# Two-layer hybrid decoder with experts: in a gather, both of ScalarE's writes ahead of both of VectorE's

## The chip, the cores and the metric

The kernel runs on one core of one Trainium2 chip. The metric is the device time of one execution in microseconds (us). The engines are TensorE (PE in the profile, with its weight loads as PEld), VectorE (DVE), ScalarE (ACT), GpSimd (POOL) and SyncE (SP), which issues the transfers.

## The reference, cut to what matters

There are 256 tokens of width 1024 and two layers. Each layer has a mixer and a feed-forward part. In the second layer the feed-forward part is eight experts, of which each token uses two:

```python
logits = (t @ w_router).astype(jnp.float32)
top_v, top_i = lax.top_k(logits, TOP_K)              # 2 of 8
top_w = jax.nn.softmax(top_v, axis=-1)
...
for e in range(N_EXPERTS):
    out = out + gates[:, e:e + 1] * _swiglu(t, w_g[e], w_u[e], w_d[e])
```

`_swiglu` is `(silu(t @ w_g) * (t @ w_u)) @ w_d`, with weights of 1024 x 2816, 1024 x 2816 and 2816 x 1024 for each expert, all in float32.

## The kernel before, in words

**Precision.** A float32 number is held as two parts that TensorE can multiply fast: a high part, written by ScalarE as a copy into the type float32r, and a low part, which VectorE computes as the number minus its high part. The helper `split` (L124) issues the two: ScalarE at L125, VectorE at L127. A full product is three matmuls (`mm3`, L184 high by high, L185 high token by low weight, L186 low token by high weight).

**Weights.** They stream from HBM in chunks of 1 MB (128 x 2048). `weights` (L137) issues the load on SP into a buffer `w` or `wx` and then splits it into `wr` and `wl` (every fourth chunk into `wrx` and `wlx`): one ScalarE and one VectorE instruction for each chunk. There are 33 chunks for each expert. Chunks are asked for three ahead of TensorE (`fetch`, `AHEAD = 3`); the parts stand in three slots `wr`/`wl` and one slot `wrx`/`wlx`.

**Experts.** They are sorted by how many tokens chose them and taken in four pairs p = 0 to 3, one heavy expert (up to 128 tokens) and one light one (up to 64 tokens). The heavy one costs three matmuls (L184 to L186), the light one two (L888, L889), since the high and the low parts of its 64 tokens stand beside each other in one operand of 128 columns.

**The gather.** The tokens of a pair are brought together by `pick` (L812): matmuls of the tokens with a 0/1 matrix (L821) into a PSUM bank `gb`, two slices of 128 features in one bank, columns 0 to 127 for the heavy expert's tokens and 128 to 191 for the light one's. Then `gb` is split into the tile `xg`: `xg[:, 0]` has the heavy high parts, `xg[:, 1]` the heavy low parts, `xg[:, 2]` both parts of the light tokens. One call of `pick` handles one bank, so a pair takes four calls (here: groups 0 to 3). For pair 0 the heavy and the light part are picked by separate calls. For pairs 1, 2 and 3 one call does both, so there are 3 x 4 = 12 calls with two splits.

**Order.** The program is a list of steps: a chunk's matmuls, and between them jobs such as the gather of the pair after next (`chunk`, `collect`). It is recorded in `in_order()`, which keeps TensorE, ScalarE and VectorE each in the order in which the code is written. So an instruction that waits holds up all that stands behind it on its engine. The framework adds the semaphore waits between engines from the tiles that instructions read and write, and it also keeps two engines out of one PSUM bank.

Of the kernel before, what the change touches and what calls it, by code (L numbers as in the profile page):

```python
# [8 lines left out]
F32 = mybir.dt.float32  # L9
# [3 lines left out]
AF = mybir.ActivationFunctionType  # L13
ALU = mybir.AluOpType
# [3 lines left out]
P = 128  # L18
# [7 lines left out]
FEW = 64  # L26
# [86 lines left out]
def trunk_kernel(ctx: ExitStack, tc: tile.TileContext, x, w_in, w_out, dense_w_gate, dense_w_up, dense_w_down,  # L113
                 moe_w_gate, moe_w_up, moe_w_down, final_norm_g, consts, decay_w, out):
    nc = tc.nc
# [8 lines left out]
    def split(src, r, l, scale=1.0):  # L124
        i0 = nc.scalar.activation(r, src, AF.Copy, scale=scale)  # L125
        if isinstance(scale, float) and scale == 1.0:
            i1 = nc.vector.tensor_tensor(l, src, r.bitcast(F32), op=ALU.subtract)  # L127
        else:
            i1 = nc.vector.scalar_tensor_tensor(l, src, scale, r.bitcast(F32), op0=ALU.mult, op1=ALU.subtract)
        return i0, i1  # L130
# [66 lines left out]
    def bank(shape, name):  # L197
        return ps.tile(shape, F32, name=name, tag="ps")
# [449 lines left out]
    def moe(l, j, accs):  # L648
# [7 lines left out]
        for tt in range(TT):  # L656
            for nh in range(2):
# [4 lines left out]
                for kt in range(4 * nh, 4 * nh + 4):  # L662
# [4 lines left out]
                                   op=ALU.subtract)  # L667
# [144 lines left out]
        def pick(p, c0, c1, groups=range(KT // 2)):  # L812
            xg, oh = X[p][0:2]
            for k2 in groups:
                b = bank([P, 2, 2 * P], "gb")
                for i in range(2):
                    kt = 2 * k2 + i
                    n = 0
                    for tt in range(TT):
                        for xs in (xr, xl):  # L820
                            nc.tensor.matmul(b[:, i, c0:c1], xs[:, tt, kt * P:(kt + 1) * P],  # L821
                                             oh[:, tt].rearrange("p a b -> p (a b)")[:, c0:c1],
                                             start=(n == 0), stop=(n == 3))
                            n += 1
                ks = slice(2 * k2, 2 * k2 + 2)
                if c0 == 0:
                    split(b[:, :, 0:P], xg[:, 0, ks], xg[:, 1, ks])
                if c1 > P:
                    split(b[:, :, P:P + FEW], xg[:, 2, ks, 0:FEW], xg[:, 2, ks, FEW:P])

        def space(p):
            t = tmp([P, 4, KT, P], "xg", tag="A" if p % 2 == 0 else "E", bufs=1, dt=F32R)
# [129 lines left out]
        def scale(e, nhs=(0, 1)):  # L962
            gs = X[e // 2][2][e % 2][:, 0:1]
            if 0 in nhs:
                G[e] = tmp([P, 2, 2, 512], "yg", tag="gy", bufs=1, dt=F32R)
            for nh in nhs:
                last = split(Y[e][nh], G[e][:, 0, nh], G[e][:, 1, nh], scale=gs)
            return last
# [29 lines left out]
        def collect(p):  # L998
            jobs.extend([(space, p), (marks, p, 0), (marks, p, 1)])
            jobs.extend([(factors, p, 0), (factors, p, 1), (back, p)])  # L1000
            jobs.extend((pick, p, 0, P + FEW, (k2,)) for k2 in range(KT // 2))

        count, order, assign, where, shares, limits = places()
        jobs.extend([(count,), (order,), (assign,), (where,), (marks, 0, 1), (shares,)])
        jobs.extend((pick, 0, P, P + FEW, (k2,)) for k2 in range(KT // 2))
        jobs.extend([(factors, 0, 1), (back, 0), (limits,)])
        n_pairs = len(items[0]) + LAG
# [48 lines left out]
        space(0)  # L1056
        put = marks(0, 0)
        pick(0, 0, P)
        hold(2, (msk_set, last_x), (put,))
        with behind((put,)):  # L1060
# [11 lines left out]
        low = scale(NE - 1)  # L1072
# [142 lines left out]
```

## Time and profile before

| | us |
|---|---|
| median of 3 runs | 1178.57 |
| lowest and highest of them | 1177.09 and 1180.01 |
| the profiled execution's own time | 1178.44 |
| its span (first to last instruction) | 1176.6 |
| the experts' part in it | from about 441 on |

The span is what the trace shows; 1.84 us of the profiled execution's time lie around it. Columns of rows below that come from a timeline: start in us from the span's start, duration in us, engine, line, operation, output<-inputs, shape, count, and in brackets how long the engine stood idle ahead of the row and what ended that. Matmuls overlap, so what a matmul costs is read from one start to the next.

### The profile page before, as it was taken

How to read it: one execution, taken by the hardware profiler on the slowest of the kernel's cores; microseconds unless marked ns; L12 is line 12 of the kernel's file. 1: busy time of each engine (PE TensorE's matmuls, PEld its weight loads, DVE VectorE, ACT ScalarE, POOL GpSimd, SP SyncE). 2: the span in 40 equal slices, each digit the busy share in tenths (PEclk: the TensorE clock that was granted, in tenths of full speed). 3: DMA queues.
4: the chain of work that ended last, by engine and by line, in shares of the span. 5: the costliest groups of instructions: out<-in, count | busy, mean ns of one | idle time of the engine just before them, and what ended most of it. 6: DMA issues, size and time to landing. Idle time of an engine off the chain costs nothing.

```text
span 1176.6 us, 17161 instructions
## 1 busy us (share of the span) xinstructions
PE 1135.7 (97%) x6633; PEld 989.5 (84%) x6633; DVE 991.0 (84%) x1065; ACT 788.6 (67%) x801; POOL 28.1 (2%) x36
## 2 busy tenths in 40 slices
PE   6999999999899999999989999999999999999995
PEld 6998999999799978888868888878888878888883
DVE  4998655555679876899889999979999979999996
ACT  5754544334455466688678887778887778887873
POOL 2001000000000120000000000000000000000000
PEclk9999999999999998999999999999999999999998
DMA  9333455455433455998989999989999989999991
GB/s 377 129 139 149 184 190 198 180 179 179 163 133 137 180 215 204 369 383 322 368 323 414 391 424 389 417 319 410 392 424 389 408 322 409 393 424 389 425 386 38
DMA packets 48934, 348.97 MB, mean 297 GB/s; under 512 B 5447, under 2 KB 5447, under 8 KB 7120
## 3 DMA queue, kind: packets, MB, share of 16 engines
q1 hardware_dynamic: 48384, 345.50, 74.5%
q0 software_dynamic: 464, 2.33, 0.5%
q8 instruction: 54, 0.88, 0.3%
q14 instruction: 32, 0.26, 0.1%
HBM read 346.76 MB, written 1.05 MB: 296 GB/s over the span
## 4 chain that ended last, share of the span: by engine, by line
PE 88%; DVE 5%; ACT 3%; issue 2%; DMA 1%; POOL 0%; SPq 0%; POOLq 0%; ACTq 0%; DVEq 0%
PE gu L186 10%; PE gu L184 10%; PE gu L185 10%; PE acc_y L184 6%; PE acc_y L186 6%; PE acc_y L185 6%; PE gu L888 6%; PE gu L889 6%; DVE wl L127 3%; PE acc_y L957 3%; PE fb L930 3%; PE acc_y L958 3%; PE sbk L445 1%; ACT wr L125 1%; PE a_ps L191 1%
## 5 line engine op out<-in xcount | busy, mean ns | idle before, releaser
L127 DVE TENSOR_TENSOR wl<-w,wr 128x2048 fp32r<-128x2048 f32 (+2 forms) x267 | 464.5, 1762 | 68.0 <-ACT wr L125 67.6
L125 ACT ACTIVATE wr<-w 128x2048 fp32r<-128x2048 f32 (+2 forms) x267 | 391.7, 1490 | 186.8 <-issue 108.9
L127 DVE TENSOR_TENSOR wl<-wx,wr 128x2048 fp32r<-128x2048 f32 x54 | 123.0, 2287 | 9.6 <-ACT wr L125 9.5
L186 PE MATMUL gu<-wr,xg 128*128 128x512 f32 (+1 forms) x296 | 112.5, 380 | 2.0 <-DVE xg L127 2.0
L185 PE MATMUL gu<-wl,xg 128*128 128x512 f32 (+1 forms) x296 | 112.3, 379 | 1.9 <-DVE wl L127 1.8
L184 PE MATMUL gu<-wr,xg 128*128 128x512 f32 (+1 forms) x296 | 113.9, 385 | 0.0
L125 ACT ACTIVATE wr<-wx 128x2048 fp32r<-128x2048 f32 x54 | 102.5, 1910 | 7.5 <-PE gu L186 3.4
L127 DVE TENSOR_TENSOR wlx<-w,wrx 128x2048 fp32r<-128x2048 f32 x45 | 102.8, 2286 | 5.1 <-ACT wrx L125 5.0
L888 PE MATMUL gu<-wr,xg 128*128 128x512 f32 (+1 forms) x288 | 106.4, 377 | 0.0
L889 PE MATMUL gu<-wl,xg 128*128 128x512 f32 (+1 forms) x288 | 104.5, 370 | 0.0
L184 PE MATMUL gu<-f,wr 128*128 128x256 f32 x336 | 95.1, 283 | 0.0
L185 PE MATMUL gu<-f,wr 128*128 128x256 f32 x336 | 95.0, 283 | 0.0
L186 PE MATMUL gu<-f,wl 128*128 128x256 f32 x336 | 95.0, 283 | 0.0
L185 PE MATMUL acc_y<-wl,hr 128*128 128x512 f32 x228 | 90.0, 395 | 0.6 <-DVE wl L127 0.6
L184 PE MATMUL acc_y<-wr,hr 128*128 128x512 f32 x228 | 90.3, 396 | 0.0
L186 PE MATMUL acc_y<-wr,hl 128*128 128x512 f32 x228 | 89.9, 394 | 0.0
L125 ACT ACTIVATE wrx<-w 128x2048 fp32r<-128x2048 f32 x45 | 86.3, 1918 | 3.1 <-PE gu L186 1.8
L185 PEld LDWEIGHTS gu<-wl,xg 128*128 128x128 f32 x296 | 57.1, 193 | 12.8 <-DVE wl L127 2.7
L186 PEld LDWEIGHTS gu<-wr,xg 128*128 128x128 f32 x296 | 56.8, 192 | 13.0 <-DVE xg L127 2.4
L184 PEld LDWEIGHTS gu<-wr,xg 128*128 128x128 f32 x296 | 56.9, 192 | 10.8 <-ACT xg L125 0.6
L185 PEld LDWEIGHTS gu<-f,wr 128*128 128x128 f32 x336 | 64.4, 192 | 0.4
L184 PEld LDWEIGHTS gu<-f,wr 128*128 128x128 f32 x336 | 64.4, 192 | 0.4
(341 smaller groups left out, 2415.6 us busy)
## 6 DMA issues: line engine op xcount, KB each, us to landing
w<-in_moe_w_gate_dram SPq DMA_DIRECT2D x64, 1024.0 KB, 7.3
w<-in_moe_w_up_dram SPq DMA_DIRECT2D x60, 1024.0 KB, 7.4
w<-in_moe_w_down_dram SPq DMA_DIRECT2D x59, 1024.0 KB, 7.4
wx<-in_moe_w_down_dram SPq DMA_DIRECT2D x25, 1024.0 KB, 7.6
wx<-in_moe_w_gate_dram SPq DMA_DIRECT2D x24, 1024.0 KB, 7.2
wx<-in_moe_w_up_dram SPq DMA_DIRECT2D x23, 1024.0 KB, 7.3
w<-in_w_in_dram SPq DMA_DIRECT2D x20, 1024.0 KB, 4.7
w<-in_dense_w_gate_dram SPq DMA_DIRECT2D x11, 1024.0 KB, 4.9
```

Of the source, the lines that this page charges most:

```text
L125: i0 = nc.scalar.activation(r, src, AF.Copy, scale=scale)
L127: i1 = nc.vector.tensor_tensor(l, src, r.bitcast(F32), op=ALU.subtract)
L184: nc.tensor.matmul(o, sr, mr, start=start, stop=False)
L185: nc.tensor.matmul(o, sr, ml, start=False, stop=False)
L186: nc.tensor.matmul(o, sl, mr, start=False, stop=stop)
L191: nc.tensor.matmul(o, s[:, kt], m[:, kt], start=(n == 0 and kt == 0), stop=(n == 2 and kt == KT - 1))
L445: nc.tensor.matmul(o, a0, a1, start=True, stop=True)
L888: nc.tensor.matmul(o, xg[:, 2, kt], wr[:, i], start=(kt == 0), stop=False)
L889: nc.tensor.matmul(o, xg[:, 2, kt], wl[:, i], start=False, stop=(kt == KT - 1))
L930: nc.tensor.matmul(b[:, n, i], kept[n][:, i * P:(i + 1) * P], X[e // 2][4], start=True, stop=True)
L957: nc.tensor.matmul(Y[e][nh], hb, wr[:, i, cs], start=first, stop=False)
L958: nc.tensor.matmul(Y[e][nh], hb, wl[:, i, cs], start=False, stop=fin)
```

## The change

`pick` no longer calls `split` for the heavy and then for the light columns. It collects the one or two parts, has ScalarE write all high parts, and then has VectorE write all low parts. The operations, shapes and operands are the same.

```diff
                 ks = slice(2 * k2, 2 * k2 + 2)
+                parts = []
                 if c0 == 0:
-                    split(b[:, :, 0:P], xg[:, 0, ks], xg[:, 1, ks])
+                    parts.append((b[:, :, 0:P], xg[:, 0, ks], xg[:, 1, ks]))
                 if c1 > P:
-                    split(b[:, :, P:P + FEW], xg[:, 2, ks, 0:FEW], xg[:, 2, ks, FEW:P])
+                    parts.append((b[:, :, P:P + FEW], xg[:, 2, ks, 0:FEW], xg[:, 2, ks, FEW:P]))
+                for o, r, _ in parts:
+                    nc.scalar.activation(r, o, AF.Copy)
+                for o, r, low in parts:
+                    nc.vector.tensor_tensor(low, o, r.bitcast(F32), op=ALU.subtract)
```

ScalarE's instructions around group 3 of pair 1's gather, before. The names in brackets are the semaphores that an instruction waits for: PE, DVE and Activation are the engines, DMAHW a transfer. The first two rows are the heavy and the light high parts.

```order
L125 ACTIVATE xg<-gb 128x256 [waits PE_49]
L125 ACTIVATE xg<-gb 128x2x64 [waits DVE_49]
L125 ACTIVATE hr<-tb 128x256 [waits PE_49]
L125 ACTIVATE wr<-w 128x2048 [waits DMAHW1_49,Activation_49]
L125 ACTIVATE wr<-w 128x2048 [waits DMAHW2_49,PE_49,Activation_49]
```

The same place after the change (lines below the edit are five higher):

```order
L832 ACTIVATE xg<-gb 128x256 [waits PE_49]
L832 ACTIVATE xg<-gb 128x2x64
L125 ACTIVATE hr<-tb 128x256 [waits PE_49]
L125 ACTIVATE wr<-w 128x2048 [waits DMAHW1_49,DVE_49]
L125 ACTIVATE wr<-w 128x2048 [waits DMAHW2_49,DVE_49,PE_49]
```

No row has moved: on each engine the order is as before in the whole program. What differs is the waits. The light high part no longer waits for VectorE. The wait of the weight copies for VectorE is now written out; it is for the last VectorE instruction that read their slot, which is several chunks back and was covered by the light part's wait before.

VectorE's instructions at the same place, before: two weight chunks, the heavy and the light low parts, another job's low part, and the next chunk.

```order
L127 TENSOR_TENSOR wlx<-w,wrx 128x2048 [waits DMAHW7_49,DVE_49,Activation_49]
L127 TENSOR_TENSOR wl<-w,wr 128x2048 [waits DMAHW0_49,DVE_49,Activation_49]
L127 TENSOR_TENSOR xg<-gb,xg 128x256 [waits Activation_49]
L127 TENSOR_TENSOR xg<-gb,xg 128x2x64 [waits Activation_49]
L127 TENSOR_TENSOR hl<-tb,hr 128x256 [waits Activation_49]
L127 TENSOR_TENSOR wl<-w,wr 128x2048 [waits DMAHW1_49,DVE_49,Activation_49]
```

And after:

```order
L127 TENSOR_TENSOR wlx<-w,wrx 128x2048 [waits DMAHW7_49,Activation_49]
L127 TENSOR_TENSOR wl<-w,wr 128x2048 [waits DMAHW0_49,Activation_49]
L834 TENSOR_TENSOR xg<-gb,xg 128x256 [waits PE_49,Activation_49]
L834 TENSOR_TENSOR xg<-gb,xg 128x2x64
L127 TENSOR_TENSOR hl<-tb,hr 128x256 [waits Activation_49]
L127 TENSOR_TENSOR wl<-w,wr 128x2048 [waits DMAHW1_49,Activation_49]
```

Again no row has moved. The heavy low part now waits until ScalarE has written the light high part too, and the light low part waits for nothing of its own.

## Rows read from the trace of the kernel before

**Rows 1.** The page's first part: busy us (share of the span) x instructions.

```profile
PE 1135.7 (97%) x6633; PEld 989.5 (84%) x6633; DVE 991.0 (84%) x1065; ACT 788.6 (67%) x801; POOL 28.1 (2%) x36
```

**Rows 2.** Stretches: length, busy us of each engine, TensorE's granted clock, transfers' share, GB/s.

```profile
606.00:752.00 146.00, 146.00 (x723) 122.53 (x722) 142.19 (x96) 120.36 (x93) 0.00 (x0) 1.00 1.00 403
602.00:606.00 4.00, 4.00 (x11) 3.13 (x12) 4.00 (x2) 3.39 (x2) 0.00 (x0) 0.57 0.72 262
779.20:783.00 3.80, 3.77 (x10) 2.95 (x11) 1.16 (x4) 3.30 (x6) 0.00 (x0) 0.58 1.00 395
956.50:960.00 3.50, 3.42 (x10) 2.56 (x11) 1.03 (x4) 2.95 (x5) 0.00 (x0) 0.62 1.01 426
```

**Rows 3.** For whom ScalarE waited, 530 to 1176 us: total us, times, longest us.

```profile
ACT xg L125 <- DVE xg L127: 27.2, 12, 2.8
```

**Rows 4.** ScalarE in order of time, groups 2 and 3 of pair 1's gather.

```profile
589.70 0.28 ACT L125 ACTIVATE xg<-gb 128x128 fp32r<-128x128 f32 x1 [2.83 <-DVE xg L127]
...
590.35 1.92 ACT L125 ACTIVATE wrx<-w 128x2048 fp32r<-128x2048 f32 x1
592.16 1.90 ACT L125 ACTIVATE wr<-w 128x2048 fp32r<-128x2048 f32 x1
593.96 0.38 ACT L125 ACTIVATE xg<-gb 128x256 fp32r<-128x256 f32 x1
597.16 0.28 ACT L125 ACTIVATE xg<-gb 128x128 fp32r<-128x128 f32 x1 [2.83 <-DVE xg L127]
597.33 0.38 ACT L125 ACTIVATE hr<-tb 128x256 fp32r<-128x256 f32 x1
597.59 3.71 ACT L125 ACTIVATE wr<-w 128x2048 fp32r<-128x2048 f32 x2
```

**Rows 5.** VectorE in order of time, the same place.

```profile
592.29 2.29 DVE L127 TENSOR_TENSOR wlx<-w,wrx 128x2048 fp32r<-128x2048 f32 x1 [2.00 <-ACT wrx L125]
594.50 2.28 DVE L127 TENSOR_TENSOR wl<-w,wr 128x2048 fp32r<-128x2048 f32 x1
596.71 0.42 DVE L127 TENSOR_TENSOR xg<-gb,xg 128x256 fp32r<-128x256 f32 x1
597.47 0.29 DVE L127 TENSOR_TENSOR xg<-gb,xg 128x128 fp32r<-128x128 f32 x1 [0.34 <-ACT xg L125]
...
599.54 4.49 DVE L127 TENSOR_TENSOR wl<-w,wr 128x2048 fp32r<-128x2048 f32 x2 [1.38 <-ACT wr L125]
```

**Rows 6.** TensorE in order of time, pair 1's gather: its start, waits and end.

```profile
583.34 0.41 PE L184 MATMUL acc_y<-wr,hr 128*128 128x512 f32 x1
...
594.64 0.50 PE L889 MATMUL gu<-wlx,xg 128*128 128x512 f32 x1 [1.45 <-DVE wlx L127]
...
601.89 0.50 PE L185 MATMUL gu<-wl,xg 128*128 128x512 f32 x1 [1.82 <-DVE wl L127]
...
606.10 1.11 PE L930 MATMUL fb<-fold,kept 128*128 128x64 f32 x9
```

**Rows 7.** TensorE in order of time, pair 2's gather.

```profile
767.14 1.04 PE L821 MATMUL gb<-xg,xt 128*128 128x192 f32 x8
...
773.66 0.41 PE L184 MATMUL gu<-wr,xg 128*128 128x512 f32 x1
...
776.44 0.50 PE L184 MATMUL gu<-wrx,xg 128*128 128x512 f32 x1
...
779.23 0.50 PE L186 MATMUL gu<-wrx,xg 128*128 128x512 f32 x1 [2.04 <-DVE xg L127]
...
783.20 1.02 PE L930 MATMUL fb<-fold,kept 128*128 128x64 f32 x8
```

**Rows 8.** TensorE in order of time, pair 3's gather.

```profile
951.06 0.41 PE L184 MATMUL gu<-wr,xg 128*128 128x512 f32 x1
...
956.58 0.50 PE L186 MATMUL gu<-wr,xg 128*128 128x512 f32 x1 [2.04 <-DVE xg L127]
...
960.42 2.04 PE L930 MATMUL fb<-fold,kept 128*128 128x64 f32 x16
```

## The prediction

> **What bounds the kernel now.** I read the busy shares first, then the stretches, the list of whom ScalarE waits for, and last the three engines side by side through the gathers. TensorE is busy for 97% of the span and VectorE for 84% [rows 1], so time can be won only where TensorE stands still or runs slowly. Between two gathers it does neither: from 606 to 752 us it is busy for 146.00 of 146 us at granted clock 1.00, which is the 2.4 GHz level, and VectorE keeps up beside it [rows 2]. In the gathers it does both. In pair 1's gather it waits 1.45 and 1.82 us for low parts of weights [rows 6]; in pair 2's and pair 3's it waits 2.04 us each for a low part of the gathered tokens [rows 7, 8]. Right behind the longest wait of each gather the granted clock is 0.57, 0.58 and 0.62, so for most of that stretch it is at the 1.2 GHz level [rows 2].
>
> Why VectorE is late there shows on the other two engines. ScalarE copies the heavy high part, then wants to copy the light one, and stands still until VectorE has done the heavy low part: 12 times, 27.2 us together, 2.27 us on average [rows 3]. In group 3 of pair 1 it is ready for the light part soon after 593.96 and starts it at 597.16; two weight copies stand behind it and start at 597.59 [rows 4]. VectorE, still at an earlier weight chunk, reaches the heavy low part at 596.71, ends it at 597.13, and then lacks work itself: 0.34 us until the light high part is there, then 1.38 us (2.00 us one group earlier) until the weight copy that ScalarE could not start is done [rows 5]. So a small read of a PSUM bank couples the two engines in both directions: ScalarE waits for the late VectorE, and VectorE is made later by that.
>
> **The change, part by part.** No instruction is added, removed or moved within its engine. Twelve waits of ScalarE for VectorE go; twelve waits of VectorE become longer.
>
> *What TensorE loses now*, as the actual time from start to start less that at full clock. The price at full clock is 2.78 us for 12 matmuls of 512 columns (773.66 to 776.44), 0.232 each [rows 7].
> - Pair 1: from 583.34 to 606.10 are 22.76 us [rows 6]. They hold 64 matmuls of 512 columns (two heavy down chunks, two light and two heavy gate or up chunks), 64 x 0.232 = 14.83, and one gather group with two transposes, for which I take the 1.04 us of a gather row [rows 7]. That makes 15.87, so 6.89 us are lost.
> - Pair 2: from 776.44 to 783.20 are 6.76 us for 12 matmuls [rows 7], 3.98 lost.
> - Pair 3: from 951.06 to 960.42 are 9.36 us for 24 matmuls [rows 8], 5.56 at full clock, 3.80 lost.
>
> Together 14.67 us. Of this the half clock is 4.00 x 0.43 + 3.80 x 0.42 + 3.50 x 0.38 = 4.65 us [rows 2]; the rest is waiting and starting up again.
>
> *Whether all of it goes.* ScalarE now goes on at once to the light part and the weight copies, so VectorE finds its inputs ready. In the group shown it saves 0.34 + 1.38 = 1.72 us [rows 5]; four such groups are 6.9 us, as much as TensorE loses in the worst gather. What is late next is checked at the two tightest places, with row durations added in full, although rows overlap a little:
> - Pair 1, the chunk that is waited for at 601.89. Without waits TensorE ends the fourth gather group at 583.34 + 24 x 0.232 + 1.04 = 589.9. Then ScalarE's heavy and light part and the other job behind them take 0.38 + 0.28 + 0.38, the weight copy 1.92 [rows 4], VectorE's low part 2.29 [rows 5]: ready at 595.2. TensorE wants it after 28 more matmuls of 512 columns and one, 589.9 + 29 x 0.232 = 596.6. Lead 1.4 us.
> - Pair 2, the low part that is waited for at 779.23, of group 2. Group 1's product is there at 767.14 + 1.04 = 768.2 [rows 7]. ScalarE: 1.04 as above and a copy of 1.92 [rows 4]; VectorE: two chunks of 2.29 and the heavy low part, 0.42 [rows 5]: ready at 776.1. TensorE wants it two matmuls after 776.44, at 776.9. Lead 0.8 us. Pair 3 has the same order.
>
> So TensorE should wait at neither, and then nothing that the trace shows lowers its clock there. After a gather, the stretch from 606 to 752 starts now with VectorE just in time and still has no wait [rows 2]; with a lead it has none the more.
>
> *What the change costs.* The heavy low part starts after the light high part, about 0.28 + 0.03 = 0.31 us later where VectorE is early: the light part's row is 0.28 us long, and from its end at 597.44 to VectorE's next start are 0.03 us [rows 4, 5]. Where VectorE is late, as the mean wait of 2.27 us says it mostly is [rows 3], that is covered. Bounds: nothing, and 12 x 0.31 = 3.7 us if ScalarE always came last and each delay reached TensorE. I take nothing, for both leads above have the light part in them.
>
> *A rule that speaks against this.* In the trace the light copy starts 0.03 us after the heavy low part ends, at 597.16 and 597.13 [rows 4, 5], though neither reads what the other writes. The Trainium skill says why (PSUM — Partial Sum Buffer, PSUM bank collisions raise a hardware error): two engines must not be in one bank at the same time, reads included, and the compiler's scheduler sets a dependency between them, ScalarE against VectorE too; the trace agrees. By the rule the exclusion is not removed but turned round, and VectorE now pays it. Priced at its full 3.7 us the gain would be 11.0 and the time 1167.6; by the rows it is covered, and the gain is 14.7.
>
> **The sum.** Span 1176.6 - 14.67 = 1161.9; with the 1.84 us around it 1163.8 for an execution such as the profiled one, whose 1178.44 lies 0.13 us under the median. So 1164 for the median of 1178.57.
>
> **The rivals.**
> - *Only weight waits go* (8%). TensorE's two waits for gathered tokens stay, since ScalarE cannot copy a group before TensorE has made it, and a lead of 0.8 us is small. It decides if the chain from group 1 to group 2's low part takes 0.8 us more than its rows. Then 3.98 + 3.80 stay and the time is 1178.6 - 6.9 = 1171.7. For it: those waits end on a token part, not on a weight [rows 7, 8]. Against: the chain was summed with full durations.
> - *The transfers become the bound* (4%). A pair's 66 chunks are 69.2 MB; at 403 GB/s, the rate at transfer share 1.00 [rows 2], they take 171.7 us. From 773.66 to 951.06 are 177.4 us now, and 173.6 without pair 3's loss. If the sustained rate were 395 GB/s [rows 2], 175.2 us, each pair could gain only 2.2, three of them 6.6: 1172. Against: at share 1.00 TensorE waited for nothing [rows 2].
> - *No effect* (5%): ScalarE's wait is idle time of an engine with room, VectorE is late through its own work, and the wait for a light part turns into one for a full weight slot or for a gather not yet made. Then 1178.6. For it: ScalarE is busy for 67% only [rows 1]. Against: VectorE's 1.38 and 2.00 us end on ScalarE's weight copies [rows 5].
> - *Slower* (3%): ScalarE, not VectorE, is last at each heavy low part, and the 0.31 us reach TensorE 12 times, 3.7 us: 1182.3. It decides once ScalarE's light part ends after VectorE has come to the bank in nearly every group. Against: before, ScalarE is the one that waits in all 12 [rows 3].
>
> **How the numbers follow.** All waits going has 80%, with its own range 1161.5 to 1167 (a median moves by some 1.5 us, as the runs shown do, and the leads are small). The range 1161.5 to 1172.5 takes in the first two rivals and leaves out the last two, 8%. A change under 0.3% (3.5 us) can't be told from none. The first three cases, 92%, are faster by more; no effect is 5%; slower is 3%.
>
> **What would show it.** Right: no ScalarE row on `xg` that waits for VectorE; the light part directly behind the heavy one; no TensorE wait over 0.5 us from 580 to 1100 and a granted clock of 1.00 in all three gathers; the start of pair 3's gather about 11 us earlier. Wrong: ScalarE waits of 2 us for `gb` with VectorE idle behind them; waits of TensorE for `xg` at pairs 2 and 3; transfers landing after ScalarE wants them.

## The result, and the profile after

The changed kernel takes 1164.36 us (median of 5 runs, 1163.78 to 1165.30). The kernel before, run beside it, takes 1179.24 us (5 runs, 1177.09 to 1180.87). The ratio is 0.9875 (95% interval 0.9861 to 0.9890). Forecast were 1164.0 us and a range of 1161.5 to 1172.5. The profiled execution took 1163.78 us with a span of 1162.0, against 1178.44 and 1176.6 before.

The first part of the page, busy time of each engine, has the same counts as before [rows 1]:

```profile
PE 1129.8 (97%) x6633; PEld 988.3 (85%) x6633; DVE 989.3 (85%) x1065; ACT 788.9 (68%) x801; POOL 28.1 (2%) x36
```

TensorE is busy for 5.9 us less than the 1135.7 of before, with as many products: some run faster. The other 8.7 of the 14.6 us by which the span became shorter are idle time.

TensorE in order of time, changed kernel, pair 1's gather from its start to the end of the chunk that was waited for [rows 6], then the ends of the gathers of pairs 2 and 3 [rows 7, 8]:

```profile
583.50 0.41 PE L184 MATMUL acc_y<-wr,hr 128*128 128x512 f32 x1
...
596.85 0.39 PE L185 MATMUL gu<-wl,xg 128*128 128x512 f32 x1
...
599.34 1.89 PE L935 MATMUL fb<-fold,kept 128*128 128x64 f32 x16
...
769.67 0.40 PE L184 MATMUL gu<-wrx,xg 128*128 128x512 f32 x1
...
770.14 0.39 PE L186 MATMUL gu<-wrx,xg 128*128 128x512 f32 x1
...
772.44 1.23 PE L935 MATMUL fb<-fold,kept 128*128 128x64 f32 x10
...
940.28 0.41 PE L184 MATMUL gu<-wr,xg 128*128 128x512 f32 x1
...
945.75 0.44 PE L935 MATMUL fb<-fold,kept 128*128 128x64 f32 x3
```

No row has a bracket, so TensorE waits at none of them; between 560 and 1110 us the trace lists no wait of a product of TensorE. The same work as in rows 6 to 8 takes 599.34 - 583.50 = 15.84 us (before 22.76), 772.44 - 769.67 = 2.77 (6.76) and 945.75 - 940.28 = 5.47 (9.36). The gains are 6.92, 3.99 and 3.89, together 14.80 us.

Busy time, granted clock (the column behind POOL), share and rate of the transfers in four stretches of the changed kernel: the ends of the three gathers, and the long stretch between two gathers.

```profile
599.34:745.00 145.66, 145.66 (x721) 122.23 (x720) 142.01 (x95) 120.13 (x92) 0.00 (x0) 1.00 1.00 405
595.00:599.00 4.00, 4.00 (x19) 3.30 (x18) 4.00 (x3) 3.74 (x3) 0.00 (x0) 1.00 0.98 381
772.00:776.00 4.00, 4.00 (x27) 3.61 (x26) 2.54 (x2) 2.31 (x3) 0.00 (x0) 1.00 0.98 389
945.00:949.00 4.00, 4.00 (x28) 3.58 (x27) 2.90 (x3) 2.15 (x4) 0.00 (x0) 1.00 1.02 401
```

Where 0.57, 0.58 and 0.62 stood behind the waits [rows 2], there is now 1.00, the 2.4 GHz level. The long stretch still runs without a wait, and the transfers at 405 GB/s keep up with it.

Whom ScalarE waits for between 560 and 1110 us (total us, times, longest), and ScalarE in order of time at group 3 of pair 1:

```profile
ACT xg L832 <- PE gb L821: 8.8, 10, 1.8
```

```profile
590.19 0.55 ACT L832 ACTIVATE xg<-gb 128x256 fp32r<-128x256 f32 x2 [1.75 <-PE gb L821]
590.63 0.39 ACT L125 ACTIVATE hr<-tb 128x256 fp32r<-128x256 f32 x1
590.89 3.73 ACT L125 ACTIVATE wr<-w 128x2048 fp32r<-128x2048 f32 x2
```

The 12 waits for VectorE [rows 3] are gone. The heavy and the light copy are one row of two (x2), and the weight copies start 0.70 us after the first of them; before it was 3.63 us [rows 4]. In their place ScalarE, now early, waits 10 times for the gather's product (before: 3 times, 1.3 us).

VectorE at the same place, and then at group 2 of pair 2:

```profile
591.00 0.62 DVE L834 TENSOR_TENSOR xg<-gb,xg 128x256 fp32r<-128x256 f32 x2
591.53 0.41 DVE L127 TENSOR_TENSOR hl<-tb,hr 128x256 fp32r<-128x256 f32 x1
592.85 4.50 DVE L127 TENSOR_TENSOR wl<-w,wr 128x2048 fp32r<-128x2048 f32 x2 [0.91 <-ACT wr L125]
...
768.53 1.15 DVE L834 TENSOR_TENSOR xg<-gb,xg 128x256 fp32r<-128x256 f32 x4
```

The low parts follow each other without a wait; the wait for the weight copy has shrunk from 1.38 to 0.91 us [rows 5]. Whom VectorE waits for from 560 to 1110 us, the rows on weight copies and on `xg`, before and then after:

```profile
DVE wl L127 <- ACT wr L125: 16.8, 16, 2.0
DVE wlx L127 <- ACT wrx L125: 8.4, 5, 2.0
DVE xg L127 <- ACT xg L125: 5.1, 14, 0.5
...
DVE wl L127 <- ACT wr L125: 13.1, 14, 1.4
DVE wlx L127 <- ACT wrx L125: 2.3, 2, 1.4
```

The waits for weight copies fell from 25.2 to 15.4 us together. No row for `xg` is left: VectorE comes to the bank after both high parts are written, so the wait that the change adds is nowhere paid. The margin is thin: in group 3 of pair 1 the high parts end at 590.19 + 0.55 = 590.74 and VectorE starts at 591.00.

### The profile page after: what moved, and what is told of

Same layout as the page of the kernel before. It is cut to its first block, busy times and chain, and to the rows that moved or that the text cites. A ratio compares the mean times of both kernels' runs of the same rounds, so it can differ in the third digit from the quotient of the medians.

```text
span 1162.0 us, 17163 instructions
## 1 busy us (share of the span) xinstructions
PE 1129.8 (97%) x6633; PEld 988.3 (85%) x6633; DVE 989.3 (85%) x1065; ACT 788.9 (68%) x801; POOL 28.1 (2%) x36
## 4 chain that ended last, share of the span: by engine, by line
PE 93%; DVE 3%; ACT 1%; issue 1%; DMA 1%; POOL 0%; SPq 0%; POOLq 0%; ACTq 0%; DVEq 0%
PE gu L184 10%; PE gu L186 10%; PE gu L185 10%; PE acc_y L184 7%; PE acc_y L186 6%; PE acc_y L185 6%; PE gu L893 6%; PE gu L894 6%; PE acc_y L962 3%; PE acc_y L963 3%; PE fb L935 3%; PE gb L821 2%; PE sbk L445 1%; DVE wl L127 1%; PE a_ps L191 1%; PE cb L981 1%
## 5 line engine op out<-in xcount | busy, mean ns | idle before, releaser
L184 PE MATMUL gu<-wr,xg 128*128 128x512 f32 (+1 forms) x296 | 112.0, 378 | 0.0
L186 PE MATMUL gu<-wr,xg 128*128 128x512 f32 (+1 forms) x296 | 110.5, 373 | 0.0
L893 PE MATMUL gu<-wr,xg 128*128 128x512 f32 (+1 forms) x288 | 106.3, 377 | 0.0
L186 PEld LDWEIGHTS gu<-wr,xg 128*128 128x128 f32 x296 | 56.0, 189 | 10.4
L186 PEld LDWEIGHTS gu<-f,wl 128*128 128x128 f32 x336 | 64.4, 192 | 0.0
```

The lines of the kernel that those rows point to most:

```text
L184: nc.tensor.matmul(o, sr, mr, start=start, stop=False)
L186: nc.tensor.matmul(o, sl, mr, start=False, stop=stop)
L893: nc.tensor.matmul(o, xg[:, 2, kt], wr[:, i], start=(kt == 0), stop=False)
```

## The experiments

The theory: ScalarE, held at the light high part, cannot start the weight copies behind it, and the three losses in the gathers come from that, each by itself. The main rivals: the order on VectorE (two low parts behind each other) does it; or the gain of one gather depends on the others; or the wait turned round costs VectorE something that was merely hidden. Diffs are against the changed kernel unless said otherwise. "Under" and "over" are differences of medians to 1164.36.

**The new order in pair 1 only.**

```diff
-                for o, r, _ in parts:
-                    nc.scalar.activation(r, o, AF.Copy)
-                for o, r, low in parts:
-                    nc.vector.tensor_tensor(low, o, r.bitcast(F32), op=ALU.subtract)
+                for some in ([parts] if p == 1 else [[part] for part in parts]):
+                    for o, r, _ in some:
+                        nc.scalar.activation(r, o, AF.Copy)
+                    for o, r, low in some:
+                        nc.vector.tensor_tensor(low, o, r.bitcast(F32), op=ALU.subtract)
```

> The new order in the gather of pair 1 alone; pairs 2 and 3 keep the old one. Theory (each gather's coupling of ScalarE and VectorE costs by itself, sized by TensorE's loss there): 6.9 us of the gain come, 7.8 us stay out, so about 1172 where before is 1179 and the change 1164.4; TensorE waits about 2 us for xg at pairs 2 and 3 as before, and the clock falls behind both. Rival (once VectorE gets a lead at one gather it keeps it to the next): pairs 2 and 3 lose their waits too, 1164 to 1166.

Measured: 1173.19 us (5 runs, 1172.42 to 1174.31), ratio 0.9945 (0.9931 to 0.9958). From 560 to 1110 us TensorE waits exactly twice, at the known places of pairs 2 and 3:

```profile
774.84 0.50 PE L186 MATMUL gu<-wrx,xg 128*128 128x512 f32 x1 [2.04 <-DVE xg L835]
...
952.21 0.50 PE L186 MATMUL gu<-wr,xg 128*128 128x512 f32 x1 [2.04 <-DVE xg L835]
```

So 6.1 us come from pair 1 alone (6.5 by the ratio; 6.9 were expected). In this run's trace pair 1's gather takes 601.74 - 585.90 = 15.84 us, as in the changed kernel, and the other two gathers have the waits that they had before: a gather's loss is its own.

**The new order, but ScalarE still waits.** Behind the two high parts ScalarE copies one column of the heavy low part into a scrap tile that nothing uses, so it stands until VectorE has written that part. The result is computed as before.

```diff
+                if len(parts) == 2:
+                    seen = tmp([P, 1], "seen", tag="seen", bufs=2)
+                    nc.scalar.activation(seen, parts[0][2].bitcast(F32)[:, 1, P - 1:P], AF.Copy)
```

> The new order, but behind the two high parts ScalarE reads one column of the heavy low part into a scrap tile, so it stands still until VectorE has written that part, as it did before the change, while VectorE's two low parts stand back to back. Theory (the gain is ScalarE going on to the weight copies): VectorE again waits 1 to 2 us for a weight copy in each group, only the 0.34 us between the low parts are saved; TensorE's waits come back, a little shorter, 1172 to 1178. Rival (the gain is VectorE's two low parts back to back): no wait comes back beyond the 0.2 us of the added instruction, 1164 to 1166.

Measured: 1178.67 us (11 runs, 1175.01 to 1180.17), ratio 0.9990 (0.9978 to 1.0003), no change from before and 0.7 us over the 1172 to 1178 expected. The list of ScalarE's waits and VectorE's rows in order of time:

```profile
ACT seen L837 <- DVE xg L834: 25.5, 12, 2.7
```

```profile
591.15 0.61 DVE L834 TENSOR_TENSOR xg<-gb,xg 128x256 fp32r<-128x256 f32 x2
594.14 2.29 DVE L127 TENSOR_TENSOR wlx<-w,wrx 128x2048 fp32r<-128x2048 f32 x1 [2.37 <-ACT wrx L125]
```

VectorE writes both low parts in one go here, and that is worth nothing: it waits 2.37 us for the next weight copy, where it waited 2.00 at that place before [rows 5]. What it saved between the low parts (0.34 us before) only moved there, and that is why the expected small gain didn't come. TensorE's waits are back too: 1.4 and 1.8 us for weights in pair 1, 2.0 us each for tokens in pairs 2 and 3. Give ScalarE its wait back and the whole gain is gone.

**The old order, without ScalarE's wait.** Against the kernel before: in the 12 gather groups with two parts VectorE writes the light high part as well.

```diff
-                if c1 > P:
+                if c1 > P and c0 == 0:
+                    nc.vector.tensor_copy(xg[:, 2, ks, 0:FEW], b[:, :, P:P + FEW])
+                    nc.vector.tensor_tensor(xg[:, 2, ks, FEW:P], b[:, :, P:P + FEW],
+                                            xg[:, 2, ks, 0:FEW].bitcast(F32), op=ALU.subtract)
+                elif c1 > P:
                     split(b[:, :, P:P + FEW], xg[:, 2, ks, 0:FEW], xg[:, 2, ks, FEW:P])
```

> The old order, but in the 12 gathers with two parts VectorE writes the light high part as well, so ScalarE has nothing to wait for in the bank and goes on to the weight copies, while VectorE has a third write of about 0.3 us between the heavy and the light low part. Theory (what counts is that ScalarE is not held up): VectorE gives 12 x 0.3 = 3.6 us of its time and that is covered as in the change, so 1164 to 1166. Rival (the order of the writes itself, high parts first and low parts together, is what pays): most of the gain stays out, 1172 and up.

Measured: 1164.12 us (4 runs, 1163.97 to 1164.52), ratio 0.9871 (0.9857 to 0.9886), the same as the change, although VectorE has 12 instructions more (and ScalarE 12 fewer) and the parts come in the old order. With the run above this settles the cause: what costs is ScalarE standing in line, not the order of the four writes.

**How much lead there is.** ScalarE writes the light high part again, 4, 7 or 12 extra times into the same place, before VectorE may come. The values don't change; only the way to the low parts gets longer. (In the diff, 4.)

```diff
+                if len(parts) == 2:
+                    for _ in range(4):
+                        nc.scalar.activation(parts[1][1], parts[1][0], AF.Copy)
```

> The new order, with the light high part copied five times over by ScalarE ahead of VectorE's low parts (four copies more, about 0.2 to 0.3 us each, 0.8 to 1.2 us a group). Theory (the heavy low part's later start is covered by a lead of about 1.2 us in pairs 2 and 3 and 1.7 us in pair 1): no change, 1164 to 1165.5. Rival (that start is on the path): 12 x 0.8 us or more, 1174 and up.

Measured: 1164.30 us (4 runs, 1162.20 to 1166.43), ratio 0.9869 (0.9854 to 0.9884). Four copies more in each of the 12 gather groups are free: VectorE waits for them in two groups, 1.2 us together, and TensorE has no wait from 560 to 1110 us. So ScalarE's own time isn't what counts either.

> As the run before with twelve copies more, 2.4 to 3.4 us a group. Theory: the leads of 1.2 and 1.7 us are used up, so TensorE waits 1 to 2 us in each gather, and where the wait is near 2 us the clock falls behind it: 1168 to 1176. Rival that the lead is larger than worked out (weight slots or the bank decide, not ScalarE's time): no change, 1164 to 1165.5.

Measured: 1198.49 us (5 runs, 1194.97 to 1200.63), ratio 1.0157 (1.0141 to 1.0172), 34 us over. The expectation missed by far. TensorE's listed waits from 560 to 1110 us sum to some 22 us; how the rest divides was not worked out, but the mean granted clock of the profiled execution is 0.977, where it is 0.989 with the change. In pair 2 TensorE now waits three times in a row, first for the gather itself:

```profile
780.19 1.11 PE L821 MATMUL gb<-xg,xt 128*128 128x192 f32 x8 [1.60 <-DVE xg L837]
...
787.91 0.50 PE L186 MATMUL gu<-wrx,xg 128*128 128x512 f32 x1 [3.38 <-DVE xg L837]
...
792.55 0.79 PE L186 MATMUL gu<-wrx,xg 128*128 128x512 f32 x1 [2.53 <-DVE xg L837]
```

> The new order with seven light copies more, which are 0.30 us each in the other two runs of this kind, so 2.1 us a group. Theory (leads of about 1.2 us in pairs 2 and 3 and 1.7 us in pair 1, each measured from the product of the group before): the copies exceed the leads by 0.9, 0.9 and 0.4 us and with 0.25 us for each new start of TensorE the time is about 3 us over the change, 1166 to 1170. Rival that the copies of all four groups add up: 4 x 2.1 = 8.4 us a gather less the lead, 7 us for each of three gathers, 1180 and more.

Measured: 1175.85 us (10 runs, 1171.51 to 1177.16), ratio 0.9962 (0.9948 to 0.9976), 11.5 us over. Neither expectation held. ScalarE and VectorE in order of time in pair 2's gather, and TensorE in pairs 2 and 3:

```profile
775.56 0.56 ACT L832 ACTIVATE xg<-gb 128x256 fp32r<-128x256 f32 x2
776.15 2.13 ACT L835 ACTIVATE xg<-gb 128x128 fp32r<-128x128 f32 x7
```

```profile
778.31 0.62 DVE L837 TENSOR_TENSOR xg<-gb,xg 128x256 fp32r<-128x256 f32 x2 [2.47 <-ACT xg L835]
```

```profile
775.70 0.50 PE L186 MATMUL gu<-wrx,xg 128*128 128x512 f32 x1 [1.09 <-DVE xg L837]
...
778.79 0.50 PE L186 MATMUL gu<-wrx,xg 128*128 128x512 f32 x1 [1.44 <-DVE xg L837]
...
787.55 0.39 PE L965 MATMUL acc_y<-wr,hb 128*128 128x512 f32 x1
...
955.27 0.50 PE L186 MATMUL gu<-wr,xg 128*128 128x512 f32 x1 [1.08 <-DVE xg L837]
...
958.37 0.49 PE L186 MATMUL gu<-wr,xg 128*128 128x512 f32 x1 [1.43 <-DVE xg L837]
...
963.97 0.40 PE L965 MATMUL acc_y<-wrx,hb 128*128 128x512 f32 x1
```

In pairs 2 and 3 the first wait has about the size that the lead gives: a dose (what the extra copies of one group take) of 2.13 us less 1.2 us of lead (worked out below) is 0.9, and 1.09 is measured. What I had left out is that a dose is paid in every group, and groups 2 and 3 follow each other closely: group 3's copies stand behind group 2's, and TensorE waits a second time, 1.44 us. In pair 1 it waits three times for low parts of weights, 0.20, 0.69 and 1.25 us, where one wait of 0.4 was expected. The seven waits that the trace lists in the three gathers sum to 7.18 us of the 11.5. A further part is the clock, and only behind pair 2, as the last section shows.

**The same pattern at the end.** In the changed kernel's tail stand the only large waits that TensorE has left from 560 us on. ScalarE there, in order of time, and TensorE:

```profile
1129.73 0.42 ACT L125 ACTIVATE hb<-s 128x256 fp32r<-128x256 f32 x1 [2.48 <-DVE s L938]
1130.06 1.90 ACT L125 ACTIVATE wr<-wx 128x2048 fp32r<-128x2048 f32 x1
```

```profile
1134.33 0.50 PE L963 MATMUL acc_y<-wl,hb 128*128 128x512 f32 x1 [1.04 <-DVE wl L127]
...
1143.20 0.50 PE L962 MATMUL acc_y<-wrx,hb 128*128 128x512 f32 x1 [1.80 <-DVE hb L127]
...
1144.45 0.63 PE L962 MATMUL acc_y<-wrx,hb 128*128 128x512 f32 x1
...
1146.15 1.65 PE L981 MATMUL cb<-yg,xg 128*128 128x512 f32 x4
```

ScalarE's copy in `unfold` waits 2.48 us for VectorE's row in `fold` (L938), with a weight copy standing behind it: the gathers' fault once more. Two edits, of order alone: (a) in the closing round `unfold` is written behind the next chunk, so that weight copies go ahead of it; (b) the additions into `h` (`finish`) of the last heavy expert are written behind the last light expert's `unfold`, so that they don't stand ahead of its low parts on VectorE.

```diff
-                jobs.extend((finish, e, (tt,), (nh,)) for nh in range(2) for tt in range(TT))
+                (tail if e == NE - 2 else jobs).extend((finish, e, (tt,), (nh,)) for nh in range(2) for tt in range(TT))   # (b)
...
-            if lt1:
+            if lt1 and not closing:                 # (a)
                 step(unfold, *lt1)
+            if lt1 == items[1][-1]:                 # (b)
+                for job in tail:
+                    step(*job)
...
             if lt_:
                 step(proj(0, *lt_))
+            if lt1 and closing:                     # (a)
+                step(unfold, *lt1)
```

> The change, with the same idea at the program's end, where ScalarE waits 2.5 and 3.7 us for VectorE's product of the folded columns with a weight copy behind it: in the closing round the split of the folded columns is recorded behind the next chunk, and the four additions of the last heavy expert's result come after the last split instead of between the last weight chunks. Theory (an instruction that waits for a late engine holds up the copies behind it): TensorE's waits of 1.0 and 1.8 us at the end go or shrink, 1.5 to 2.5 us less than the change. Rival (VectorE is the bound at the end whatever the order, since a light chunk takes it longer than TensorE): no change.

Measured with both: 1158.25 us (5 runs, 1158.14 to 1160.04), ratio 0.9826 (0.9813 to 0.9839). This version beats both kernels. The size was off: 6.1 us under, not 1.5 to 2.5. So the edits were run alone.

> One of the two edits of the tail alone: in the closing round the last heavy expert's unfold is written behind the next chunk's weight copies. In the changed kernel's trace ScalarE waits there 2.48 us for VectorE's row on s at 1129.73 with a weight copy queued behind it, which is the pattern of the gathers again. Theory (that wait is the larger part of the 6.1 us that both edits gave): TensorE's wait of 1.04 us at 1134.33 goes, the wait at 1143.20 shrinks from 1.80 us to about 0.6 to 1.2 (the additions into h still stand ahead of the last low part), 1159.5 to 1161.5 us. Rival (the additions are the larger part): 1162.5 to 1164 us.

> The other edit of the tail alone: the additions of the last heavy expert into h are written behind the last light expert's unfold. Theory: two additions of 0.6 us leave VectorE's way ahead of the last light low parts, TensorE's wait at 1143.20 shrinks from 1.80 us to about 0.6, the wait of 1.04 us at 1134.33 stays, 1162 to 1163.5 us. Rival (the additions are the larger part of the 6.1 us): 1158.5 to 1161 us, with the half clock at the end gone too.

Measured: (a) alone 1159.58 us (5 runs, 1159.56 to 1161.58), ratio 0.9836 (0.9820 to 0.9851); (b) alone 1161.16 us (5 runs, 1160.43 to 1162.52), ratio 0.9846 (0.9830 to 0.9861), between what the two expectations gave. By the ratios to 0.9875 that is 4.6 and 3.4 us, and 5.8 for both: less than their sum, though each ratio is uncertain by some 1.6 us. The profiled executions show the same from the same row near the end (`fb`, eight products, at 1124.41 in the changed kernel) to the end of the span: 37.59 us with the change, 33.62 with (a), 34.15 with (b), 32.06 with both, which are gains of 3.97, 3.44 and 5.53. TensorE in order of time with (a) alone:

```profile
1140.84 0.50 PE L962 MATMUL acc_y<-wrx,hb 128*128 128x512 f32 x1 [1.18 <-DVE hb L127]
...
1141.41 0.40 PE L962 MATMUL acc_y<-wrx,hb 128*128 128x512 f32 x1
...
1142.81 1.09 PE L981 MATMUL cb<-yg,xg 128*128 128x512 f32 x4
```

With (a) the wait of 1.04 us is gone and that of 1.80 is 1.18, as expected. But the products behind it also run at full rate: the eight of the last chunk take 1142.81 - 1140.84 = 1.97 us, where they took 1146.15 - 1143.20 = 2.95, and the four `cb` products after them 1.09 us instead of 1.65. Together that is 1.54 us of clock. With (b) the wait of 1.80 us goes altogether and the wait for `wl` is 1.51 us, since the two additions' products no longer stand ahead of it:

```profile
1135.08 0.50 PE L963 MATMUL acc_y<-wl,hb 128*128 128x512 f32 x1 [1.51 <-DVE wl L127]
...
1141.87 2.01 PE L981 MATMUL cb<-yg,xg 128*128 128x512 f32 x8
```

Here too the last chunk runs at full rate. Either edit wins the clock back, and it can be won only once: 1.54 of the 1.88 us by which the two gains of the profiled executions exceed that of both. The clock is one term that I had left out of the 1.5 to 2.5 us. A second is in the row at 1141.87: with (b) all eight products of the heavy expert's additions run ahead of the last chunk, where TensorE had waited, and the four of 1146.15 no longer stand behind it. What each term gives of the 5.8 us with both was not separated.

## Why the prediction was right

*What TensorE loses.* The three terms were 6.89, 3.98 and 3.80 us; 6.92, 3.99 and 3.89 came back. The way of working them out, the actual time from start to start less the number of products at the full-clock price, holds to 0.1 us in each. The prediction named two waits in pair 1; the trace of the kernel before lists a third, 0.63 us for a low part of weights at 587.18, which the time from start to start has in it.

*Whether all of it goes.* Pair 1's chunk is ready when the first of its two weight rows ends, at 592.85 + 2.29 = 595.14, and TensorE wants it at 596.85: a lead of 1.7 us where 1.4 was worked out. In pair 2 four low parts start at 768.53; the first of them, group 2's heavy one, takes 0.42 us [rows 5] and is done by 768.95, and TensorE wants it at 770.14: a lead of 1.2 where 0.8 was worked out. Both estimates were low, because row durations were added in full, as the prediction said. Its other argument, four groups at 1.72 us, gave TensorE's loss in pair 1 partly by luck: VectorE's listed waits for ScalarE from 570 to 606 us fell from 8.4 to 3.3 us, by 5.1 and not by 6.9.

*What the change costs.* Taken as nothing, and nothing it is: no wait of VectorE for `xg` is left, and even four more copies in each gather group change nothing (1164.30 us). The Trainium skill's rule on banks (PSUM — Partial Sum Buffer, PSUM bank collisions raise a hardware error), by which engines that share a bank are kept apart by a dependency, agrees with the trace: with seven extra copies VectorE's heavy low part starts at 778.31, when the last light copy ends (776.15 + 2.13 = 778.28), 2.47 us after VectorE was free. The four writes of a group also share the tile `xg`, but that isn't what keeps the engines apart: in the changed kernel's pair 2 ScalarE writes group 3's high parts into the same tile, from another bank, while VectorE comes to group 2's low parts only at 768.53:

```profile
767.12 0.58 ACT L832 ACTIVATE xg<-gb 128x256 fp32r<-128x256 f32 x2
```

The exclusion is thus turned round, as the prediction put it; it costs once it is longer than the lead.

*The rivals.* Only weight waits go: excluded by rows 769.67 to 772.44, without a wait. The transfers as the bound: excluded by the stretch at 405 GB/s in which TensorE never waits. (The prediction took pair 3's loss out of the 177.4 us from pair 2's gather to pair 3's; it is pair 2's that lies in them, which leaves 173.4, and 940.28 - 766.90 = 173.38 us were measured. The rival's time doesn't hang on it.) No effect, and slower: excluded by the time. The two runs that separate ScalarE's wait from the order of the writes (1178.67 and 1164.12 us) show the mechanism itself, not only its time.

*The signs.* Pair 3's gather starts 951.06 - 940.28 = 10.8 us earlier (about 11 forecast). One sign that had been listed as speaking against it did appear in part: ScalarE waits up to 1.8 us for `gb`, and behind one such wait in each gather (1.74 to 1.76 us) VectorE stands 0.89 to 0.92 us. It reaches no one: in pairs 1 and 2, where the leads above have it in them, 1.7 and 1.2 us are left, and in pair 3 no product of TensorE waits. Such a wait is the sign of an engine that is early, and it tells something only with the lead beside it.

*The half clock* was counted as 4.65 of the 14.67 us. TensorE's busy time fell by 5.9 us; that the products are faster is shown by it, and the size agrees roughly, since a product behind a wait counts as busy for longer (0.50 us for 0.39, as the rows with brackets show). No run took away the waits of the changed gathers and left the half clock there.

## What to carry to other kernels

Where engines take their work in order, ask of each wait not what it costs its own engine but what stands behind it: 27 us of waits of an engine that was 67% busy held up weight copies, and removing them gave 14.7 us. Write all that the early engine has to do on a shared bank first, and only then what the late engine does; the price is a longer way to the late engine's first write, which is free as long as it is under the lead at the tightest place. That lead can be measured by repeating a small instruction, but for the whole row of groups that follow each other, not for one.

## What the runs showed of the hardware that was not expected

**The clock after the same two waits.** With seven extra copies, pairs 2 and 3 have the same waits (1.09 and 1.44 us; 1.08 and 1.43) and the same products behind them. Their granted clock right behind, in that kernel's stretches:

```profile
779.82:783.20 3.38, 3.38 (x19) 3.28 (x18) 3.09 (x2) 3.23 (x5) 0.00 (x0) 0.62 0.19 73
...
958.00:962.00 4.00, 3.63 (x24) 3.33 (x25) 2.82 (x4) 4.00 (x4) 0.00 (x0) 1.00 0.35 141
```

Pair 2 falls to the 1.2 GHz level for most of the stretch, pair 3 stays at 2.4 GHz. From the second wait's end to the thirteenth `acc_y` product pair 2 takes 787.55 - 778.79 = 8.76 us and pair 3 963.97 - 958.37 = 5.60. So the half clock alone costs 3.16 us here, and the waits alone don't decide whether it comes. What does is open. The Trainium skill (TensorE: Matmul & The Clock Gate, Part 1, on the clock gate) says that the monitor behind the clock looks at windows that run freely, so that the loss differs between runs of one kernel; the two pairs agree with that, and no run here sets their place against such a window. That kernel's ten runs lie in two groups, 1171.5 to 1173.1 and 1175.7 to 1177.2 us, with a mean granted clock of 0.988 to 0.989 and 0.985 to 0.986; one more or one less such stretch would explain a step of about that size, which is argued and not shown.

**Equal copies behind each other.** The light copy's row is 0.28 us, and ScalarE's next instruction starts 0.17 us after it [rows 4]. Repeated into the same place, seven copies take 2.13 us and twelve 3.67, 0.30 us each. Twelve copies were therefore a dose of 3.67 us; 12 x 0.17 would be 2.0, and 2.4 to 3.4 had been expected. That is a small part of the miss with twelve. Why equal copies stand further apart was not tried.
